# Layer 0's out projection by column halves with kept weights, its LayerNorms on VectorE alone, and normalised rows in the residual's tiles

## The chip, the cores and the metric

The kernel runs on one core of a Trainium2 chip. Its engines work side by side and meet through semaphores: TensorE (PE) multiplies, with a queue of its own for weight loads (PEld); VectorE (DVE), ScalarE (ACT) and GpSimd (POOL) do elementwise work; SyncE (SP) issues most of the DMAs. Each engine takes its instructions strictly in the order in which they were written for it. The metric is the device time of one execution in microseconds (us), as a median of runs.

## The reference

Two layers of a diffusion backbone on 256 context tokens and 256 latent tokens of width 1024. What matters here is layer 0 from its output projection on; both streams pass through the same weights, with modulation rows of their own:

```
y     = mixed @ w_out                                   # 1024 x 1024
x_mid = LN(alpha * x + ada2 * y) * ln1_g + ln1_b
h2    = LN(x_mid) * (1 + ada4) + ada3                   # "modulate"
f     = (silu(h2 @ wg) * (h2 @ wu)) @ wd                # 1024 -> 2816 -> 1024
x     = LN(alpha * x_mid + ada5 * f) * ln2_g + ln2_b
h     = LN(x) * (1 + ada1) + ada0                       # layer 1 begins, then h @ w_in
```

Everything is float32. LN is a LayerNorm without gain and bias.

## The kernel before, in words

The 512 tokens are four tiles of 128 rows: tiles 0 and 1 are the context (stream s=0), tiles 2 and 3 the latent tokens (s=1). A row tile is two SBUF tiles of 128x512. A float32 product is made of three matmuls (`mm3`, L223 to L225): high by high, high by low, low by high part. `load_w` brings a block of a weight, here 512 rows by 256 columns (512 KB), with a DMA on SP's queue; ACT then makes the high part (L216, tile "hi") and DVE the low part (L217, tile "lo"). The weights stand in rings of tiles: raw 5, hi 3, lo 3, and in the phase "ff" 3, 1 and 1 more, so that four pairs of hi and lo exist there. A split has to wait until TensorE has read the pair that it overwrites.

A row-major product (`tok_group`) fills one PSUM bank "PM" for two token tiles and a group g of 256 output columns; there are four such groups and three PM banks. Its evacuation is `add_residual`: DVE multiplies the bank with the gate row (L1040), POOL adds the residual (L1041), DVE takes the LayerNorm statistics (L1042). `post_ln` then closes the statistics (the power -1/2 is POOL's, L231, "rs") and applies LN, gain and bias: the first 512 columns on DVE in two instructions (L1054, L1055), the last 512 on ACT (L1050) and POOL (L1051, L1052). With quick=True, which `out_last` uses in layer 1, add and both halves are DVE's.

`modulate` is next. `normalise` takes statistics again (L247) and makes the normalised row, half on ACT (L361), half on DVE (L362), into tiles of tag "B". TensorE transposes it in eight column blocks (L374, PSUM tiles "PX", three of them). Each block is scaled and shifted into a tile of the ring "sg" (ACT L382 and DVE L380 in turn), and split into high part (ACT L383) and low part (DVE L384); both go into tiles "H", which the next matmuls read.

The first place is L1690 to L1693: stream by stream, `out_proj` runs groups g=0 to 3 over two tiles (so w_out is read twice), then post LN and modulate. The second is the end of `ffn` (L1151 to L1161): for each stream the last 10 of 22 blocks of the down projection, again in four groups, into new tiles "xn" of tag "in", then post LN and modulate for layer 1, whose projection by w_in follows.

The ring "sg" has four tiles. A tile of a ring is handed out in the order in which the program asks for it; who asks waits until the last reader of the tile's former content is done. Within such bounds a scheduler writes each engine's order when the kernel is built; at run time nothing is reordered.

Of the kernel before, what the change touches and what calls it, by code (L numbers as in the profile page):

```python
# [10 lines left out]
F32 = mybir.dt.float32  # L11
# [85 lines left out]
def hybrid_backbone(ctx: ExitStack, tc: tile.TileContext, A, out, dbg=None, stop=None):  # L97
# [28 lines left out]
    def tt(tag, dt=F32, n=512):  # L126
        t = S["main"].tile([128, 512], dt, name=tag, tag=tag, bufs=TAGS[tag])
        return t if n == 512 else t[:, :n]

    def ht(dt=F32R):  # L130
        return hpool.tile([128, 512], dt, name="H")
# [101 lines left out]
    def ln_open(k):  # L233
        return cc(24, "bst", bufs=4).rearrange("p (a b) -> p a b", b=6)[:, :k]
# [15 lines left out]
    def load_row(src, tag):  # L250
        r = []
        for i in range(2):
            t = tt(tag)
            nc.gpsimd.dma_start(t, bcast_rows(src[512 * i:512 * i + 512], 512))
            r.append(t)
        return r
# [99 lines left out]
    def normalise(x):  # L356
        mu, rs = ln_stats(x)
        nb = cc(1, "nb", bufs=4)
        nc.vector.scalar_tensor_tensor(nb, mu, -1.0, rs, op0=OP.mult, op1=OP.mult)
        z = [tt("B") for _ in range(2)]  # L360
        nc.scalar.activation(z[0], x[0], AF.Identity, scale=rs, bias=nb)  # L361
        nc.vector.tensor_scalar(z[1], x[1], mu, rs, op0=OP.subtract, op1=OP.mult)  # L362
        return z
# [72 lines left out]
    def tok_group(src, c0, act, evac, tiles, n=256, kk=8):  # L436

        h, lo = act
        tiles = list(tiles)
        banks = [pmt() for _ in range(0, len(tiles), 2)]  # L440
        ps = {t: banks[i // 2][:, 256 * (i % 2):256 * (i % 2) + n] for i, t in enumerate(tiles)}
        for k0 in range(0, kk, 4):
            kc = min(4, kk - k0)
            w = load_w(src, 128 * k0, kc, c0, n)
            for i, t in enumerate(tiles):
                for k in range(kc):
                    sl = slice(128 * t, 128 * t + 128)

                    mm3(ps[t], (h[k0 + k][:, sl], lo[k0 + k][:, sl]), (w[0][:, k, :], w[1][:, k, :]),
                        k0 + k == 0 and i % 2 == 0, k0 + k == kk - 1, skip_group_check=True)  # L450
        for t in tiles:
            evac(t, ps[t])
# [583 lines left out]

    def add_residual(z, g, p, r, ax, st, quick=False):
        c = slice(256 * (g % 2), 256 * (g % 2) + 256)
        zc = z[g // 2][:, c]
        nc.vector.tensor_tensor(zc, p, r[g // 2][:, c], op=OP.mult)  # L1040
        (nc.vector if quick else nc.gpsimd).tensor_tensor(zc, zc, ax[g // 2][:, c], op=OP.add)  # L1041
        nc.vector.bn_stats(st[:, g, :], zc)  # L1042

    def post_ln(z, st, rows, quick=False):
# [12 lines left out]
    def times_alpha(x):  # L1057
        for i in range(2):
            nc.scalar.activation(x[i], x[i], AF.Copy, scale=ALPHA)
        return x  # L1060

    def out_proj(l, m, ax, s, rows):
        tiles = (2 * s, 2 * s + 1)
        zs = {t: [tt("in") if l == 0 else ht(F32) for _ in range(2)] for t in tiles}
        st = {t: ln_open(4) for t in tiles}
        r = load_row(S["adarows"][0, l, 1 - s, :], "C")
        for g in range(4):
            tok_group(A["w_out"][l], 256 * g, m, lambda t, p: add_residual(zs[t], g, p, r, ax[t], st[t]), tiles)
        for t in tiles:
            post_ln(zs[t], st[t], rows)  # L1070
        return zs

    def out_last(m, ax, rows, after):
# [22 lines left out]
    def ffn(act, xm, fill, plan, after):  # L1096

        wg, wu, wd = A["ffd_wg"][0], A["ffd_wu"][0], A["ffd_wd"][0]
        zs = {}
        hid = {}  # L1100

        def up(fp, sl):
            sgs = [None, None]

            def ev_g(i, p):
                s = sg()
                sgs[i] = s
                nc.scalar.activation(s[:, sl], p[:, sl], AF.Silu)  # L1108

            def ev_u(i, p):  # L1110
                s = sgs[i]
                nc.vector.tensor_tensor(s[:, sl], s[:, sl], p[:, sl], op=OP.mult)
                if fp + i not in hid:
                    hid[fp + i] = (tt("B", F32R), tt("C", F32R))
                hi, lo = hid[fp + i]
                nc.scalar.activation(hi[:, sl], s[:, sl], AF.Copy)
                nc.vector.tensor_tensor(lo[:, sl], s[:, sl], hi[:, sl], op=OP.subtract)
            col_pair(wg, 128 * fp, act, ev_g, sl)
            col_pair(wu, 128 * fp, act, ev_u, sl)

        def take(at):
            for _ in range(plan.count(chr(65 + at))):
                fill.pop(0)()
        for half, (f0, f1) in enumerate(((0, 12), (12, 22))):
            for fp in range(f0, f1, 2):
                if fp == 0:
                    for sl in (slice(0, 256), slice(256, 512)):
                        for f in (0, 2):
                            up(f, sl)
                elif fp > 2:  # L1130
                    up(fp, slice(0, 512))
                if fp == 4:
                    for t in range(4):
                        times_alpha(xm[t])
                take(fp // 2)
            n = f1 - f0
            hh = ([hid[f][0] for f in range(f0, f1)], [hid[f][1] for f in range(f0, f1)])
            if half == 0:
                rows = {j: load_row(S["adarows"][1, 0, j, :], "in") for j in range(2)}
                for t in range(4):  # L1140
                    zs[t] = xm[t]
                for g in range(4):
                    def ev(t, p):
                        c = slice(256 * (g % 2), 256 * (g % 2) + 256)
                        k = sg()[:, :256]
                        nc.vector.tensor_tensor(k, p, rows[0 if t >= 2 else 1][g // 2][:, c], op=OP.mult)
                        nc.gpsimd.tensor_tensor(zs[t][g // 2][:, c], zs[t][g // 2][:, c], k, op=OP.add)
                    tok_group(wd[128 * f0:128 * f1], 256 * g, hh, ev, range(4), kk=n)
                    take(11 + g)
        ln2 = load_row(A["ln2_g"][0], "B"), load_row(A["ln2_b"][0], "B")  # L1150
        for s in range(2):  # L1151
            tiles = (2 * s, 2 * s + 1)
            st = {t: ln_open(4) for t in tiles}
            xn = {t: [tt("in") for _ in range(2)] for t in tiles}
            for g in range(4):
                tok_group(wd[128 * f0:128 * f1], 256 * g, hh,
                          lambda t, p: add_residual(xn[t], g, p, rows[1 - s], zs[t], st[t]), tiles, kk=n)
                take(15 + 4 * s + g)
            for t in tiles:
                post_ln(xn[t], st[t], ln2)  # L1160
            after(s, xn)  # L1161

# [487 lines left out]
    def load_x(t, q):  # L1652
        src = A["ctx"][0, 128 * t:128 * t + 128, :] if t < 2 else A["x"][0, 128 * (t - 2):128 * (t - 2) + 128, :]
        x = [tt("in") for _ in range(2)]
        for i in range(2):
            q.dma_start(x[i], src[:, 512 * i:512 * i + 512])
        return x

    xsave = dram.tile([2, 128, D], F32, name="xsave")
    with phase("main") as S["main"]:  # L1660
# [24 lines left out]
        with phase("ff") as ff, deeper(ff, 3, 1, 1):  # L1685
            ff.tile([128, 16], F32, name="shift")
            act = new_act()
            rows = load_row(A["ln1_g"][0], "B"), load_row(A["ln1_b"][0], "B")
            xm = {}
            for s in range(2):  # L1690
                ax = {t: times_alpha(load_x(t, nc.gpsimd)) for t in (2 * s, 2 * s + 1)}
                xm.update(out_proj(0, m, ax, s, rows))
                modulate(0, xm, 3, s, act)  # L1693
            for t in range(4):
                for i in range(2):
                    dump("xmid0", xm[t][i], lambda o: o[128 * t:128 * t + 128, 512 * i:512 * i + 512])
            if stop == "mid":
                return
            act2 = []

            def after(s, x):
                if not act2:
                    act2.extend(new_act())
                for t in x:
                    for i in range(2):
                        dump("x0", x[t][i], lambda o: o[128 * t:128 * t + 128, 512 * i:512 * i + 512])
                        if t >= 2:
                            nc.gpsimd.dma_start(xsave[t - 2, :, 512 * i:512 * i + 512], x[t][i])
                modulate(1, x, 0, s, act2)
            ffn(act, xm, fill, "CDFGHIJKLMNOPR", after)  # L1710
# [54 lines left out]
```

## Time and profile before

| | |
|---|---|
| median of 3 runs | 1908.01 us (1906.63 to 1915.2) |
| profiled execution, its own time | 1905.72 us |
| its span | 1903.9 us, mean TensorE clock 0.964 |
| TensorE busy | 1777.5 us, 93% of the span |
| VectorE busy | 1249.4 us, 66% |
| ScalarE busy | 835.0 us, 44% |
| GpSimd busy | 515.6 us, 27% |
| DMA | 337.89 MB, 177 GB/s in the mean |

TensorE is busy nearly everywhere, so what counts is where it is not, and what it waits for there. A share of busy time over the whole span says nothing on the two places of the change; windows and timelines of those places do. A row of a timeline has start, length, engine, line, operation, output and inputs and, in brackets, how long the engine stood idle before it and what released it. The granted clock is the share of full speed (1.00 is 2.4 GHz, 0.50 is 1.2 GHz).

### The profile page before, as it was taken

What the parts mean: (1) busy time and instruction counts of PE and PEld (TensorE: products, weight loads), DVE (VectorE), ACT (ScalarE), POOL (GpSimd) and SP (SyncE); (2) the same over time, 40 slices, a digit from 0 to 9 for tenths busy, and PEclk for the clock granted to TensorE, in tenths of its full rate; (3) what the DMA queues carried; (4) which work ended last, traced back from release to release, by engine and by line L of the source; (5) the groups of instructions that cost most, each with busy time, mean ns of one, the idle gap of its engine ahead of it and who ended that gap; (6) DMA issues with size and microseconds to landing.
All of it is one profiled execution on the core that took longest, in us unless ns stands there. A gap on an engine that the chain in (4) does not pass through costs nothing. (4 is left out here: it accounts for less than half of the span.)

```text
span 1903.9 us, 29201 instructions
## 1 busy us (share of the span) xinstructions
PE 1777.5 (93%) x10822; PEld 1411.8 (74%) x10822; DVE 1249.4 (66%) x2029; ACT 835.0 (44%) x1430; POOL 515.6 (27%) x532
## 2 busy tenths in 40 slices
PE   6899989999999979999999989989989899999994
PEld 3777977788777968799788978878978475664731
DVE  5777767765555876757767965676867475655722
ACT  3454554434443463221233454564644374544620
POOL 2353536652202720112102730046504000001001
PEclk8998989999999979999999989999999899999997
DMA  8424321123213736545666543323528699779994
GB/s 303 138 90 144 110 89 56 46 66 118 84 54 105 228 99 189 183 149 175 228 211 202 165 139 100 112 89 106 165 70 297 210 371 343 275 273 383 377 376 179
DMA packets 243934, 337.89 MB, mean 177 GB/s; under 512 B 16008, under 2 KB 158864, under 8 KB 243784
## 3 DMA queue, kind: packets, MB, share of 16 engines
q1 hardware_dynamic: 235896, 318.86, 50.5%
q0 software_dynamic: 6128, 13.99, 2.4%
q10 hardware_dynamic: 1760, 3.09, 0.5%
q8 instruction: 87, 1.43, 0.3%
q14 instruction: 63, 0.52, 0.1%
HBM read 333.77 MB, written 2.12 MB: 176 GB/s over the span
## 5 line engine op out<-in xcount | busy, mean ns | idle before, releaser
L217 DVE TENSOR_TENSOR lo<-raw,hi 128x1024 fp32r<-128x1024 f32 (+1 forms) x370 | 456.0, 1239 | 161.8 <-ACT hi L216 159.9
L216 ACT ACTIVATE hi<-raw 128x1024 fp32r<-128x1024 f32 (+1 forms) x370 | 368.3, 1003 | 433.9 <-PE PM L225 170.2
L223 PE MATMUL PM<-H,hi 128*128 128x512 f32 (+1 forms) x1104 | 388.0, 354 | 7.5 <-ACT sg L1108 2.9
L224 PE MATMUL PM<-H,hi 128*128 128x512 f32 (+1 forms) x1104 | 386.7, 351 | 1.2 <-DVE H L384 1.1
L225 PE MATMUL PM<-H,lo 128*128 128x512 f32 (+1 forms) x1104 | 384.9, 351 | 0.0
L223 PEld LDWEIGHTS PM<-H,hi 128*128 128x128 f32 x1104 | 211.3, 192 | 44.3 <-issue 4.4
L224 PEld LDWEIGHTS PM<-H,hi 128*128 128x128 f32 x1104 | 211.5, 192 | 32.2 <-issue 2.0
L225 PEld LDWEIGHTS PM<-H,lo 128*128 128x128 f32 x1104 | 210.5, 191 | 31.8 <-issue 2.7
L332 DVE SCALAR_TENSOR_TENSOR ad<-raw,silu,ad 128x512 f32<-128x512 f32 x208 | 177.9, 875 | 35.9 <-issue 15.1
L223 PE MATMUL PM<-hi,H 128*128 128x256 f32 x432 | 127.2, 295 | 4.1 <-ACT in L529 4.1
L224 PE MATMUL PM<-lo,H 128*128 128x256 f32 x432 | 126.7, 293 | 1.9 <-DVE lo L217 1.9
L225 PE MATMUL PM<-hi,H 128*128 128x256 f32 x432 | 126.1, 292 | 0.0
L1024 POOL TENSOR_TENSOR B<-B,sg 128x512 f32<-128x512 f32 (+1 forms) x48 | 62.7, 1318 | 216.4 <-DVE sg L1023 199.6
L1521 POOL TENSOR_TENSOR yl<-sg,yh 128x512 fp32r<-128x512 f32 x17 | 24.6, 1448 | 349.9 <-ACT yh L1520 330.8
L809 POOL TENSOR_TENSOR C<-C,in 128x512 f32<-128x512 f32 (+1 forms) x64 | 82.7, 1317 | 74.8 <-ACT C L808 48.8
L1396 PE MATMUL PM<-raw,xs 128*64 128x512 f32 (+3 forms) x448 | 99.9, 565 | 0.0
L223 PE MATMUL PM<-hi,B 128*128 128x256 f32 x352 | 98.6, 280 | 0.0
L225 PE MATMUL PM<-hi,C 128*128 128x256 f32 x352 | 98.1, 279 | 0.0
L224 PE MATMUL PM<-lo,B 128*128 128x256 f32 x352 | 98.0, 278 | 0.0
L223 PEld LDWEIGHTS PM<-hi,H 128*128 128x128 f32 x432 | 86.3, 200 | 5.7 <-ACT in L529 4.3
L224 PEld LDWEIGHTS PM<-lo,H 128*128 128x128 f32 x432 | 86.4, 200 | 4.1 <-DVE lo L217 2.2
L225 PEld LDWEIGHTS PM<-hi,H 128*128 128x128 f32 x432 | 86.4, 200 | 0.8 <-issue 0.8
(444 smaller groups left out, 3561.8 us busy)
## 6 DMA issues: line engine op xcount, KB each, us to landing
raw<-in_w_ada_dram SPq DMA_DIRECT2D x80, 512.0 KB, 4.3
raw<-in_moe_wd_dram SPq DMA_DIRECT2D x80, 512.0 KB, 7.0
raw<-in_w_gate_dram SPq DMA_DIRECT2D x64, 512.0 KB, 3.6
raw<-in_moe_wg_dram SPq DMA_DIRECT2D x60, 512.0 KB, 8.2
raw<-in_moe_wu_dram SPq DMA_DIRECT2D x60, 512.0 KB, 9.9
raw<-in_w_in_dram SPq DMA_DIRECT2D x54, 512.0 KB, 3.7
raw<-in_ffd_wd_dram SPq DMA_DIRECT2D x28, 512.0 KB, 3.5
raw<-in_ffd_wg_dram SPq DMA_DIRECT2D x26, 512.0 KB, 3.8
```

What stands on the lines that cost most here:

```text
L216: nc.scalar.activation(h[:, :m], raw[:, :m], AF.Copy)
L217: (nc.vector if ahead else nc.gpsimd).tensor_tensor(l[:, :m], raw[:, :m], h[:, :m], op=OP.subtract)
L223: nc.tensor.matmul(o, ah, bh, start=start, stop=False, **kw)
L224: nc.tensor.matmul(o, ah, bl, start=False, stop=False, **kw)
L225: nc.tensor.matmul(o, al, bh, start=False, stop=stop, **kw)
L332: nc.vector.scalar_tensor_tensor(acc[j], part, sc, acc[j], op0=OP.mult, op1=OP.add)
L809: nc.gpsimd.tensor_tensor(E[:, xt], E[:, xt], X[:, xt], op=OP.mult)
L1024: nc.gpsimd.tensor_tensor(mixed[c][:, xt], mixed[c][:, xt], s[:, xt], op=OP.add)
L1396: nc.tensor.matmul(po[g, :w.shape[-1]], x[:, c, :], w, start=(c < k), stop=(c + k >= kk), tile_position=(0, g.start))
L1521: nc.gpsimd.tensor_tensor(yl, y, yh, op=OP.subtract)
```

## The change

1. `normalise` writes its rows into tiles of tag "in" instead of "B".
2. Layer 0's `out_proj` takes columns 0 to 511 (g=0, 1) for all four token tiles, with one load of the weights. It then loads the four weight blocks of columns 512 to 1023 and keeps them split, and runs g=2, 3 for s=0, then for s=1. There are 8 loads of w_out instead of 16.
3. In `out_proj` the adds of g=2, 3 and the whole post LN are DVE's (quick), and modulate of a stream follows its post LN through `after`. The x and ctx rows of all four tiles are loaded and scaled ahead of it.
4. At the end of `ffn` the tiles "xn" are gone: the sum is made in place in zs, and the product before it goes into a tile of the ring "sg". The add of g=3 and the whole post LN are DVE's.

```diff
@@ -357,7 +357,7 @@
         mu, rs = ln_stats(x)
         nb = cc(1, "nb", bufs=4)
         nc.vector.scalar_tensor_tensor(nb, mu, -1.0, rs, op0=OP.mult, op1=OP.mult)
-        z = [tt("B") for _ in range(2)]
+        z = [tt("in") for _ in range(2)]
         nc.scalar.activation(z[0], x[0], AF.Identity, scale=rs, bias=nb)
         nc.vector.tensor_scalar(z[1], x[1], mu, rs, op0=OP.subtract, op1=OP.mult)
         return z
@@ -1036,9 +1036,11 @@
 
     def add_residual(z, g, p, r, ax, st, quick=False):
         c = slice(256 * (g % 2), 256 * (g % 2) + 256)
-        zc = z[g // 2][:, c]
-        nc.vector.tensor_tensor(zc, p, r[g // 2][:, c], op=OP.mult)
-        (nc.vector if quick else nc.gpsimd).tensor_tensor(zc, zc, ax[g // 2][:, c], op=OP.add)
+        zc, k = z[g // 2][:, c], z[g // 2][:, c]
+        if z is ax:
+            k = sg()[:, :256]
+        nc.vector.tensor_tensor(k, p, r[g // 2][:, c], op=OP.mult)
+        (nc.vector if quick else nc.gpsimd).tensor_tensor(zc, k, ax[g // 2][:, c], op=OP.add)
         nc.vector.bn_stats(st[:, g, :], zc)
 
     def post_ln(z, st, rows, quick=False):
@@ -1059,15 +1061,32 @@
             nc.scalar.activation(x[i], x[i], AF.Copy, scale=ALPHA)
         return x
 
-    def out_proj(l, m, ax, s, rows):
-        tiles = (2 * s, 2 * s + 1)
-        zs = {t: [tt("in") if l == 0 else ht(F32) for _ in range(2)] for t in tiles}
-        st = {t: ln_open(4) for t in tiles}
-        r = load_row(S["adarows"][0, l, 1 - s, :], "C")
-        for g in range(4):
-            tok_group(A["w_out"][l], 256 * g, m, lambda t, p: add_residual(zs[t], g, p, r, ax[t], st[t]), tiles)
-        for t in tiles:
-            post_ln(zs[t], st[t], rows)
+    def out_proj(m, ax, rows, after):
+
+
+        w_out = A["w_out"][0]
+        zs = {t: [tt("in") for _ in range(2)] for t in range(4)}
+        st = {t: ln_open(4) for t in range(4)}
+        r = [load_row(S["adarows"][0, 0, 1 - s, :], "C") for s in range(2)]
+        for g in range(2):
+            tok_group(w_out, 256 * g, m, lambda t, p: add_residual(zs[t], g, p, r[t // 2], ax[t], st[t]), range(4))
+        w = {(g, k0): load_w(w_out, 128 * k0, 4, 256 * g, 256) for g in (2, 3) for k0 in (0, 4)}
+        for s in range(2):
+            tiles = (2 * s, 2 * s + 1)
+            for g in (2, 3):
+                ps = pmt()
+                for i, t in enumerate(tiles):
+                    o = ps[:, 256 * i:256 * i + 256]
+                    for k in range(8):
+                        wh, wl = w[g, k & 4][:2]
+                        sl = slice(128 * t, 128 * t + 128)
+                        mm3(o, (m[0][k][:, sl], m[1][k][:, sl]), (wh[:, k & 3, :], wl[:, k & 3, :]),
+                            k == 0 and i == 0, k == 7, skip_group_check=True)
+                for i, t in enumerate(tiles):
+                    add_residual(zs[t], g, ps[:, 256 * i:256 * i + 256], r[s], ax[t], st[t], quick=True)
+            for t in tiles:
+                post_ln(zs[t], st[t], rows, quick=True)
+            after(s, zs)
         return zs
 
     def out_last(m, ax, rows, after):
@@ -1151,14 +1170,13 @@
         for s in range(2):
             tiles = (2 * s, 2 * s + 1)
             st = {t: ln_open(4) for t in tiles}
-            xn = {t: [tt("in") for _ in range(2)] for t in tiles}
             for g in range(4):
                 tok_group(wd[128 * f0:128 * f1], 256 * g, hh,
-                          lambda t, p: add_residual(xn[t], g, p, rows[1 - s], zs[t], st[t]), tiles, kk=n)
+                          lambda t, p: add_residual(zs[t], g, p, rows[1 - s], zs[t], st[t], quick=g == 3), tiles, kk=n)
                 take(15 + 4 * s + g)
             for t in tiles:
-                post_ln(xn[t], st[t], ln2)
-            after(s, xn)
+                post_ln(zs[t], st[t], ln2, quick=True)
+            after(s, {t: zs[t] for t in tiles})
 
 
 
@@ -1686,11 +1704,8 @@
             ff.tile([128, 16], F32, name="shift")
             act = new_act()
             rows = load_row(A["ln1_g"][0], "B"), load_row(A["ln1_b"][0], "B")
-            xm = {}
-            for s in range(2):
-                ax = {t: times_alpha(load_x(t, nc.gpsimd)) for t in (2 * s, 2 * s + 1)}
-                xm.update(out_proj(0, m, ax, s, rows))
-                modulate(0, xm, 3, s, act)
+            xm = out_proj(m, {t: times_alpha(load_x(t, nc.gpsimd)) for t in range(4)}, rows,
+                          lambda s, zs: modulate(0, zs, 3, s, act))
             for t in range(4):
                 for i in range(2):
                     dump("xmid0", xm[t][i], lambda o: o[128 * t:128 * t + 128, 512 * i:512 * i + 512])
```

Two places of DVE's order and one of TensorE's show what moves. In what follows PM is a PSUM bank of a product, PX one of transposes, "in" a row tile.

The first is DVE in the out projection, after the normalised rows of s=0 (L362). Before:

```order
L362 TENSOR_SCALAR B_5768<-in_5453,mv_5759,rs_5761 128x512
L362 TENSOR_SCALAR B_5783<-in_5455,mv_5774,rs_5776 128x512
L217 TENSOR_TENSOR lo_6345<-raw_6342,hi_6344 128x1024
L1042 BN_STATS bst_5858<-in_5855 128x6
L1042 BN_STATS bst_5859<-in_5857 128x6
L380 TENSOR_SCALAR sg_5796<-PX_5793,adac0_119 128x256
L238 BN_AGGR mv_6132<-bst_5858 128x2
L238 BN_AGGR mv_6145<-bst_5859 128x2
```

After, where the g=2 and g=3 banks of s=1 are PM_5968 and PM_6023:

```order
L362 TENSOR_SCALAR in_5894<-in_5465,mv_5885,rs_5887 128x512
L359 SCALAR_TENSOR_TENSOR nb_5906<-mv_5900,rs_5902 128x1
L362 TENSOR_SCALAR in_5909<-in_5467,mv_5900,rs_5902 128x512
L1042 TENSOR_TENSOR in_5469<-PM_5968,C_5482 128x256
L1042 TENSOR_TENSOR in_5471<-PM_5968,C_5482 128x256
L1042 TENSOR_TENSOR in_5469<-PM_6023,C_5482 128x256
L1042 TENSOR_TENSOR in_5471<-PM_6023,C_5482 128x256
L1043 TENSOR_TENSOR in_5469<-in_5469,in_5453 128x256
L1043 TENSOR_TENSOR in_5471<-in_5471,in_5459 128x256
L1043 TENSOR_TENSOR in_5469<-in_5469,in_5453 128x256
L1043 TENSOR_TENSOR in_5471<-in_5471,in_5459 128x256
L380 TENSOR_SCALAR sg_5922<-PX_5919,adac0_119 128x256
```

Four multiplications and four adds of s=1 now stand between s=0's rows and the first of its blocks (L380); before it were a split and two statistics.

The second is DVE at the end of `ffn`. Before, PM_9834 and PM_9919 are the banks g=2 and g=3 of s=1, evacuated ahead of s=0's modulate (L380) or between its blocks:

```order
L359 SCALAR_TENSOR_TENSOR nb_9596<-mv_9590,rs_9592 128x1
L1040 TENSOR_TENSOR in_9661<-PM_9834,in_7464 128x256
L1040 TENSOR_TENSOR in_9663<-PM_9834,in_7464 128x256
L217 TENSOR_TENSOR lo_10155<-raw_10152,hi_10154 128x1024
L1042 BN_STATS bst_9658<-in_9661 128x6
L362 TENSOR_SCALAR B_9584<-in_9141,mv_9575,rs_9577 128x512
L1042 BN_STATS bst_9659<-in_9663 128x6
L362 TENSOR_SCALAR B_9599<-in_9143,mv_9590,rs_9592 128x512
L380 TENSOR_SCALAR sg_9612<-PX_9609,adac1_120 128x256
L1040 TENSOR_TENSOR in_9661<-PM_9919,in_7464 128x256
L1040 TENSOR_TENSOR in_9663<-PM_9919,in_7464 128x256
```

After, PM_9598, PM_9685 and PM_9772 are the banks g=0, 1, 2 of s=1, and L1042 is the multiplication:

```order
L384 TENSOR_TENSOR H_9506<-sg_9571,H_9498 128x256
L384 TENSOR_TENSOR H_9507<-sg_9578,H_9499 128x256
L1042 TENSOR_TENSOR sg_9677<-PM_9598,in_7402 128x256
L384 TENSOR_TENSOR H_9508<-sg_9585,H_9500 128x256
L1042 TENSOR_TENSOR sg_9681<-PM_9598,in_7402 128x256
L384 TENSOR_TENSOR H_9509<-sg_9592,H_9501 128x256
L1042 TENSOR_TENSOR sg_9764<-PM_9685,in_7402 128x256
L1044 BN_STATS bst_9596<-in_5468 128x6
L1042 TENSOR_TENSOR sg_9768<-PM_9685,in_7402 128x256
```

The multiplications of s=1's first three groups have moved behind all but the last blocks of s=0's modulate, since their products take tiles of the ring "sg" after it.

TensorE at that place. Before, the transposes (L374) stand in four lots among the last matmuls of s=1's g=3 (PM<-hi,C) and the first of w_in (PM<-H,hi); here the third and the fourth:

```order
L225 MATMUL PM<-hi,C 128x256
L374 MATMUL PX<-cst,B 128x128 x6
L223 MATMUL PM<-H,hi 128x256 x2
L223 MATMUL PM<-hi,H 128x256
L374 MATMUL PX<-cst,B 128x128 x2
L224 MATMUL PM<-H,hi 128x256
```

After, all sixteen stand in one piece ahead of s=1's g=3:

```order
L224 MATMUL PM<-lo,B 128x256
L225 MATMUL PM<-hi,C 128x256
L374 MATMUL PX<-cst,in 128x128 x16
L223 MATMUL PM<-hi,B 128x256
L224 MATMUL PM<-lo,B 128x256
```

What follows L374 is now the group g=3 itself, in a bank that g=0 held before, and no matmul of w_in stands between the transposes.

## Rows read from the trace of the kernel before

**Rows 1.** The page, busy time of each engine

```profile
PE 1777.5 (93%) x10822; PEld 1411.8 (74%) x10822; DVE 1249.4 (66%) x2029; ACT 835.0 (44%) x1430; POOL 515.6 (27%) x532
```

**Rows 2.** Windows: start:end, length, busy us of PE, PEld, DVE, ACT, POOL, clock, DMA

```profile
645.00:665.00 20.00, 20.00 (x172) 20.00 (x171) 19.11 (x38) 8.85 (x9) 15.18 (x13) 1.00 0.56 167
...
670.00:675.00 5.00, 2.68 (x11) 2.18 (x11) 5.00 (x14) 3.64 (x8) 1.71 (x2) 0.50 0.44 134
...
695.00:700.00 5.00, 2.96 (x14) 2.96 (x15) 1.94 (x6) 2.85 (x6) 0.00 (x0) 0.50 0.01 2
```

**Rows 3.** Timeline of PE, out projection to the first up matmuls

```profile
619.95 0.28 PE L223 MATMUL PM<-hi,C 128*128 128x256 f32 x1
...
665.06 0.28 PE L225 MATMUL PM<-hi,B 128*128 128x256 f32 x1
668.08 1.61 PE L374 MATMUL PX<-cst,B 128*128 128x128 f32 x6 [2.75 <-ACT B L361]
...
697.04 0.58 PE L223 MATMUL PM<-H,hi 128*128 128x256 f32 x1 [2.87 <-ACT sg L1108]
```

**Rows 4.** Timeline of DVE, same stretch

```profile
667.55 0.16 DVE L359 SCALAR_TENSOR_TENSOR nb<-mv,rs 128x1 f32<-128x1 f32 x1 [0.37 <-POOL rs L231]
...
669.93 1.21 DVE L217 TENSOR_TENSOR lo<-raw,hi 128x1024 fp32r<-128x1024 f32 x1
...
671.73 0.52 DVE L380 TENSOR_SCALAR sg<-PX,adac 128x256 f32<-128x256 f32 x1
...
672.52 0.74 DVE L1054 SCALAR_TENSOR_TENSOR in<-in,mv,B 128x512 f32<-128x512 f32 x1
...
678.97 3.29 DVE L384 TENSOR_TENSOR H<-sg,H 128x256 fp32r<-128x256 f32 x3
...
694.67 1.42 DVE L384 TENSOR_TENSOR H<-sg,H 128x256 fp32r<-128x256 f32 x4
```

**Rows 5.** Timeline of ACT, same stretch

```profile
667.22 1.52 ACT L361 ACTIVATE B<-in,nb,rs 128x512 f32<-128x512 f32 x2 [0.79 <-DVE nb L359]
...
688.19 1.14 ACT L1059 ACTIVATE in<-in 128x512 f32<-128x512 f32 x2
689.24 1.04 ACT L216 ACTIVATE hi<-raw 128x1024 fp32r<-128x1024 f32 x1
690.18 1.00 ACT L382 ACTIVATE sg<-PX,adac 128x256 f32<-128x256 f32 x2
```

**Rows 6.** Windows at the end of the feed-forward, columns as in Rows 2

```profile
1102.00:1108.00 6.00, 0.47 (x5) 0.26 (x3) 5.39 (x12) 1.30 (x3) 4.41 (x7) 0.76 0.72 206
1108.00:1112.00 4.00, 3.77 (x17) 3.17 (x18) 2.22 (x7) 3.43 (x8) 0.46 (x1) 0.51 0.63 224
```

**Rows 7.** Timeline of DVE, end of the feed-forward

```profile
1053.62 0.76 DVE L1040 TENSOR_TENSOR in<-PM,in 128x256 f32<-128x256 f32 x2
...
1100.20 4.51 DVE L217 TENSOR_TENSOR lo<-raw,hi 128x1024 fp32r<-128x1024 f32 x2
1104.64 1.27 DVE L247 BATCH_NORM_STATS2 bst<-in 128x6 f32<-128x512 f32 x2
...
1106.88 0.16 DVE L359 SCALAR_TENSOR_TENSOR nb<-mv,rs 128x1 f32<-128x1 f32 x1 [0.54 <-POOL rs L231]
...
1115.04 0.43 DVE L384 TENSOR_TENSOR H<-sg,H 128x256 fp32r<-128x256 f32 x1 [0.48 <-ACT H L383]
```

**Rows 8.** Timeline of PE, end of the feed-forward

```profile
1107.95 1.61 PE L374 MATMUL PX<-cst,B 128*128 128x128 f32 x6 [5.54 <-ACT B L361]
...
1111.83 0.40 PE L224 MATMUL PM<-H,hi 128*128 128x256 f32 x1
```

**Rows 9.** Timeline of POOL, end of the feed-forward

```profile
1086.47 2.56 POOL L1041 TENSOR_TENSOR in<-in 128x256 f32<-128x256 f32 x2
...
1096.57 3.60 POOL L1051 TENSOR_TENSOR in<-in,B 128x512 f32<-128x512 f32 x2
1100.13 3.50 POOL L1052 TENSOR_TENSOR in<-in,B 128x512 f32<-128x512 f32 x2
```

## The prediction

> **What bounds the kernel now.** I read the page first: TensorE is busy 93% of the span, no other engine over 66% [rows 1]. So only stretches in which TensorE stands still, or runs slowly, can give time or take it. The windows show two at the places of the change.
>
> Stage 1 is the end of the out projection. Its 384 matmuls run from 619.95 to 665.06 without a gap, 0.1178 us apart [rows 3], and need 45.2 us. Then TensorE waits 2.75 us for the first normalised rows (ACT L361) and is busy 2.68 us of 5 at a clock of 0.50 [rows 2, 3], fed in pieces by the modulate of s=0, then of s=1. The up matmuls after s=1's modulate begin at 697.04 [rows 3]. That instant, 77.1 us after 619.95, is my mark for stage 1. The bound is DVE: 19.11 us busy of 20 before 665, all 5 of 5 behind it [rows 2].
>
> Stage 2 is the end of the feed-forward. I count from the evacuation of s=0's last group at 1053.62 [rows 7]. TensorE works through s=1's down projection and s=0's part of w_in, then waits 5.54 us for s=1's rows (ACT L361) and runs the start of the next stretch at 0.51 [rows 6, 8]. It is back in w_in at 1111.83 [rows 8], 58.2 us after 1053.62: the mark for stage 2. The order of DVE and POOL decides here; the statistics of s=1's last columns wait for POOL's L1051 and L1052 [rows 7, 9].
>
> **The change, part by part.** The eight w_out loads that go, with 4 MB, are worth 0: TensorE waits for no weight between 619.95 and 665.06 [rows 3]. The eight splits that go with them free DVE and ACT only inside that stretch. Loading and scaling all x and ctx rows early puts four scalings of 0.57 us (two take 1.14 [rows 5]) ahead of other work of ACT; I take 0, at most 1 us if a load is late. POOL's sixteen gain and bias instructions and ACT's L1050 go. DVE gains two instructions of 0.66 us (0.74 long [rows 4], 0.08 overlapped) for each of eight half rows, 10.6 us, and 12 adds at 0.34 (four instructions on 256 columns last 1.42 [rows 4]), 4.1 us: 8.0 us in stage 1, which has eight of the adds, and 6.7 in stage 2.
>
> Stage 1. The four kept weight blocks take all four pairs of hi and lo. They are last read at 36.7, 39.6, 42.4 and 45.2 us, since s=1's two groups are the last four steps of 24 matmuls, 2.83 us each. So the next four splits, of the up weights, can't run sooner, and DVE's order has them inside s=0's post LN and statistics; the last begins after ACT's high part (1.04 [rows 5]) at 46.2 and takes 1.14 (1.21 long [rows 4]). With aggregation, power on POOL and two small instructions, 1.1 us, the factors nb stand at 48.5; before they stood at 667.55, 47.6 [rows 4]. So 0.9 us is lost, and the long LN on DVE is covered by the wait for those slots.
>
> From there DVE's order up to the nb of s=1 holds 2 L362 and 4 L380 at 0.46 (L380 is 0.52 long [rows 4]), 24 on 256 columns at 0.34 (8 multiplications and adds, 4 statistics, 8 L384, and 4 aggregations taken at half of it, 7.5 together), 8 instructions of post LN at 0.66 (5.3), 2 splits (2.3), 4 statistics on 512 columns at 0.61 (two last 1.27 [rows 7]; 2.4) and 1.2 for small ones with the power: 21.5 us, so nb is there at 70.0. ACT then makes two L361 (1.52) and four scalings (2.28) before its first L382, 73.8. In the trace the mark follows the first L382 (690.18) by 6.86 us [rows 3, 5]; so it comes at 80.7, against 77.1: **+3.6 us**. Bounds: if DVE's splits wait for TensorE and POOL's remaining adds slow it, +5.5; if DVE runs ahead into the waits of the modulate, and the scalings hide, -2.
>
> Stage 2. s=1's products now use the ring sg, whose four tiles are taken after s=0's modulate. So the evacuations of its g=0 to 2 stand behind that modulate on DVE. There are three PM banks: g=3 of s=1 can't begin before the first of them is empty, and behind it in TensorE's queue stands all of w_in. From 1053.62 TensorE has 180 matmuls, 21.2 us. DVE has, up to nb of s=0, four multiplications and adds (1.4), two statistics (0.7), 8 post LN instructions (5.3), 4 statistics on 512 (2.4), six splits at 1.14 and two of half the width (8.0), and aggregations and two powers (1.7): nb at about 19.5, 1.1 us before the second tile's. From nb to the last block of a modulate the trace has 8.6 us (1106.88 to 1115.47 [rows 7]), in part at half clock; with a split that now stands between the two tiles' factors, 9.0. So the bank is free at about 28.5. TensorE, done at 21.2 except for transposes, **waits some 6 to 7 us that are new**; before, the transposes stood between matmuls of g=3 and w_in. g=3 needs 60 matmuls, 7.1 us: 35.6.
>
> DVE's chain for s=1 from there: multiplications, adds, statistics 2.0, first four post LN instructions 2.6, five splits 5.7 of which one stands behind the copies (L532), and those wait for 96 matmuls of w_in, 11.3 us. So the copies end at 12.4, and 4 post LN instructions (2.6), a split (1.1), 4 statistics (2.4), aggregation and power (1.2) follow: nb at 19.7. TensorE's 120 matmuls of w_in end at 14.1, so it waits again. The mark followed nb (1106.88) by 4.95 us [rows 7, 8]: 35.6 + 19.7 + 4.95 = 60.3, against 58.2: +2.1. After a wait of 5.54 us the clock was 0.51 for 4 us [rows 6, 8], which would add 2 to g=3; I take half: **+3.1 us**. Bounds: -6, if the evacuations hide, as in the faster rival; +8, if g=3 runs wholly at half clock.
>
> Sum: 1905.7 + 3.6 + 3.1 = 1912.4 against the profiled execution; the median lies 2.3 above that execution, which gives 1914.7, so **1915 us**. What cannot be told from no change is 0.5%, 9.5 us: 1898.5 to 1917.5.
>
> Contention, weighed: three L384 beside POOL's L1051 and L1052 took 3.29 us, four alone 1.42 [rows 4]; two splits beside L1052 took 4.51 instead of 2.4 [rows 7]. The Trainium skill, "Trainium Architecture — The Big Picture", section "What this means for kernel authors", says that VectorE and GpSimd share a port pair with an exclusive lock. The trace agrees in these two places. That rule speaks for the change and is the first rival below.
>
> **Rivals.** Faster: without POOL's long instructions the DVE chains are shorter than before, not longer. For it: 2.2 us of excess in stage 1 and 2.1 in stage 2 by those rows; in stage 2 POOL's last add for s=1 came only at 1086.47, behind other work (its row has no idle time before it), and L1051 and L1052 held the last statistics until 1104.64 [rows 7, 9]. If the new wait at g=3 were hidden too, the 5.54 us go [rows 8], and stage 1 gains 4.3 (the excess of 2.2 and as much of half clock): 1908.0 - 9.9 = 1898. Against it: the change puts 14.7 us on DVE where 4.3 of excess go, and the evacuations behind the modulate are not a matter of speed.
>
> Slower: the clock. Place: g=3 of s=1 after the new wait, and the up matmuls after stage 1. Price: 60 matmuls wholly at half clock take 7.1 us more, of which my sum has 1, thus +6; it decides if the wait is over the 5.54 us after which 0.51 was granted [rows 6, 8], and mine is 6 or more. The up matmuls behind stage 1 would add about 2, as 4 us at half clock do: 1915 + 6 + 2 = 1923. For it: 0.50 after each wait of stage 1 [rows 2]; against it: the sixteen transposes keep TensorE partly at work during the wait. The Trainium skill, "TensorE: Matmul & The Clock Gate", section "What's actually happening", says that the throttled clock is the default and activity releases it; the trace agrees with both levels, 0.50 and 1.00.
>
> No effect at all: the slots, not DVE, set stage 1 both ways, and stage 2's wait is only moved from s=1's rows to g=3: 1908.
>
> **Chances.** Forecast and no effect together are the case within 0.5%: 0.42 (0.30 and 0.12). Slower, 0.36, is the clock rival and the upper part of my bounds; a sum along one chain leaves out the waits that it does not see. Faster, 0.22. The likeliest one's own range is 1909 to 1919; for 8 in 10 I go from 1897, the faster rival, to 1926, past the slower one.
>
> **What would show it.** Right: a wait of TensorE of 5 to 8 us before a down matmul L223, released by DVE's L1042, some 21 us after s=0's last group; the first L361 of s=0 in stage 1 a microsecond later than 2.0 us after the out projection's end; L382 of s=1 about 74 us after the projection's start; another wait of 5 us or so for L361 in w_in. Wrong: no such wait at g=3, or DVE idle before s=0's nb in stage 1; then the faster rival holds. If a clock of 0.5 stands over all of g=3, the slower one does.

## The result, and the profile after

The changed kernel takes 1923.12 us (median of 6 runs, 1922.58 to 1924.36); the kernel before took 1909.98 us over the 6 runs beside it. The ratio is 1.0067, with a 95% interval of 1.0055 to 1.0078: slower by 0.7%. The forecast was 1915 us, within 1897 to 1926; the time is that which the slower rival gave, 1923. The profiled execution took 1924.36 us, 18.6 more than that of before. Single executions scatter by some us, and the executions profiled lay low for before and high for after, so the two traces show 5.5 us more than the medians do (18.6 against 13.1).

Where the time goes can be read by following the same TensorE instruction through both traces. Up to the out projection it starts 1.9 us later after the change; both traces part near 158 us, where nothing was changed. Behind stage 1 it is 5.2 late, at the feed-forward's end 6.3, behind stage 2 14.3, and at the end 18.9. So stage 1 costs 3.3 us, stage 2 about 8, and some 4 come later, in layer 1; about 1 lies between the two stages.

**Stage 1.** The timeline of PE after the change, as in [rows 3]:

```profile
621.84 0.28 PE L223 MATMUL PM<-hi,C 128*128 128x256 f32 x1
...
666.95 0.28 PE L225 MATMUL PM<-hi,B 128*128 128x256 f32 x1
672.61 0.69 PE L374 MATMUL PX<-cst,in 128*128 128x128 f32 x2 [5.39 <-ACT in L361]
...
702.13 0.58 PE L223 MATMUL PM<-H,hi 128*128 128x256 f32 x1 [2.78 <-ACT sg L1127]
```

The projection still runs without a gap, 621.84 to 666.95, and the mark, 702.13, lies 80.3 us after its first matmul, against 77.1. The wait for s=0's rows has grown from 2.75 to 5.39 us. DVE, as in [rows 4, 5]: the evacuation of s=0's last bank, the last of the four splits for which the kept blocks hold the slots, the first factors of s=0 and of s=1. Below it ACT: the high part for that split, and its first scalings of s=1's blocks:

```profile
655.96 0.76 DVE L1042 TENSOR_TENSOR in<-PM,C 128x256 f32<-128x256 f32 x2 [3.56 <-PE PM L225]
...
669.57 1.17 DVE L217 TENSOR_TENSOR lo<-raw,hi 128x1024 fp32r<-128x1024 f32 x1
...
671.55 0.16 DVE L359 SCALAR_TENSOR_TENSOR nb<-mv,rs 128x1 f32<-128x1 f32 x1 [0.50 <-POOL rs L231]
...
692.24 0.15 DVE L359 SCALAR_TENSOR_TENSOR nb<-mv,rs 128x1 f32<-128x1 f32 x1
```

```profile
667.26 1.06 ACT L216 ACTIVATE hi<-raw 128x1024 fp32r<-128x1024 f32 x1 [0.35 <-DVE bst L247]
...
695.93 1.00 ACT L382 ACTIVATE sg<-PX,adac 128x256 f32<-128x256 f32 x2
```

Counted from the first matmul, s=0's two factors stand at 49.7 and 50.4 (before at 47.1 and 47.6; I had 48.5, set against the second), the first of s=1 at 70.4 (I had 70.0), and L382 at 74.1 (73.8). The windows show how DVE's load has moved: the first 34.1 us, up to s=0's last bank, and from there to the first factor of s=1; columns as in [rows 2]. After the change, then before it, split at the same 34.1 us:

```profile
621.84:655.94 34.10, 34.10 (x291) 34.10 (x290) 17.18 (x30) 6.01 (x7) 13.52 (x17) 1.00 0.45 140
655.94:692.24 36.30, 25.18 (x184) 23.69 (x183) 35.52 (x81) 14.76 (x24) 6.40 (x8) 0.84 0.25 73
```

```profile
619.95:654.05 34.10, 34.10 (x291) 34.10 (x290) 28.06 (x45) 16.83 (x20) 23.10 (x26) 1.00 0.75 249
654.05:684.59 30.54, 23.72 (x158) 21.98 (x157) 29.31 (x60) 15.11 (x25) 21.91 (x19) 0.78 0.41 119
```

Up to s=1's factors DVE has less work than before, 52.7 us against 57.4. But of the first 34.1 us it stands idle 16.9, before 6.0: it waits for TensorE's banks and for ACT's high parts. From s=0's last bank on it is full, 35.5 of 36.3 us, and TensorE waits for it.

**Stage 2.** DVE, as in [rows 7]: the last group of s=0, the two evacuations of the first bank of s=1, which stand among s=0's last blocks, and the first factors of s=1:

```profile
1059.88 0.76 DVE L1042 TENSOR_TENSOR sg<-PM,in 128x256 f32<-128x256 f32 x2
...
1087.43 0.42 DVE L1042 TENSOR_TENSOR sg<-PM,in 128x256 f32<-128x256 f32 x1
...
1088.09 0.42 DVE L1042 TENSOR_TENSOR sg<-PM,in 128x256 f32<-128x256 f32 x1
...
1116.90 0.16 DVE L359 SCALAR_TENSOR_TENSOR nb<-mv,rs 128x1 f32<-128x1 f32 x1 [0.61 <-POOL rs L231]
```

TensorE in the same stretch, as in [rows 8]; the rows from 1080.31 on are the transposes of s=0, 1088.57 is the first matmul of s=1's g=3:

```profile
1080.31 0.55 PE L374 MATMUL PX<-cst,in 128*128 128x128 f32 x3
1082.14 0.55 PE L374 MATMUL PX<-cst,in 128*128 128x128 f32 x3 [1.28 <-ACT in L361]
1083.13 2.02 PE L374 MATMUL PX<-cst,in 128*128 128x128 f32 x8 [0.44 <-ACT sg L382]
1085.44 0.69 PE L374 MATMUL PX<-cst,in 128*128 128x128 f32 x2 [0.30 <-ACT sg L382]
1088.57 0.58 PE L223 MATMUL PM<-hi,B 128*128 128x256 f32 x1 [2.44 <-DVE sg L1042]
...
1117.96 1.61 PE L374 MATMUL PX<-cst,in 128*128 128x128 f32 x6 [5.13 <-ACT in L361]
...
1132.87 0.50 PE L223 MATMUL PM<-H,hi 128*128 128x512 f32 x1 [1.46 <-ACT hi L216]
```

The last row has its counterpart in the kernel before:

```profile
1119.59 0.50 PE L223 MATMUL PM<-H,hi 128*128 128x512 f32 x1 [1.46 <-ACT hi L216]
```

TensorE ended s=1's g=2 at about 1080 and began g=3 at 1088.57, 28.7 us after s=0's last group; I had put that at 28.5. In the 8.6 us between it does 16 transposes and waits 4.5 us, 2.44 of them for L1042. The windows give the clock; columns as before:

```profile
1086.00:1091.00 5.00, 2.56 (x12) 2.44 (x12) 4.89 (x15) 1.37 (x5) 3.08 (x5) 0.50 0.00 0
...
1118.00:1124.00 6.00, 6.00 (x28) 5.80 (x29) 2.81 (x6) 4.30 (x10) 0.00 (x0) 0.50 0.01 2
```

g=3 begins at 0.50 and is done at 1097.85, 9.3 us instead of 7.1; and the second wait, for s=1's rows, is still there, followed by 0.50 for 6 us. The first matmul of w_in on 512 columns, which has the same work ahead of it in both kernels, starts 73.0 us after s=0's last group (1132.87), before 66.0 (1119.59): 7.0 us.

### The profile page after: what moved, and what is told of

The parts are those of the page before. It is cut to its first block, busy times and chain, and to the rows that moved or that the text cites. A ratio compares the mean times of both kernels' runs of the same rounds, so it can differ in the third digit from the quotient of the medians.

```text
span 1922.6 us, 29159 instructions
## 1 busy us (share of the span) xinstructions
PE 1786.9 (93%) x10822; PEld 1419.8 (74%) x10822; DVE 1240.7 (65%) x2041; ACT 819.0 (43%) x1414; POOL 469.6 (24%) x504
## 5 line engine op out<-in xcount | busy, mean ns | idle before, releaser
L216 ACT ACTIVATE hi<-raw 128x1024 fp32r<-128x1024 f32 (+1 forms) x362 | 360.1, 1002 | 474.8 <-PE PM L225 187.8
L217 DVE TENSOR_TENSOR lo<-raw,hi 128x1024 fp32r<-128x1024 f32 (+1 forms) x362 | 438.9, 1219 | 178.2 <-ACT hi L216 171.3
L225 PE MATMUL PM<-H,lo 128*128 128x512 f32 (+1 forms) x1104 | 387.1, 353 | 0.0
L223 PEld LDWEIGHTS PM<-H,hi 128*128 128x128 f32 x1104 | 212.8, 194 | 45.1 <-issue 6.1
L225 PEld LDWEIGHTS PM<-H,lo 128*128 128x128 f32 x1104 | 212.2, 193 | 31.6 <-issue 2.7
L225 PE MATMUL PM<-hi,H 128*128 128x256 f32 x432 | 125.6, 291 | 0.0
L225 PE MATMUL PM<-hi,C 128*128 128x256 f32 x352 | 98.9, 281 | 0.0
L225 PEld LDWEIGHTS PM<-hi,H 128*128 128x128 f32 x432 | 86.1, 199 | 0.8 <-issue 0.8
```

Source lines behind the costliest of these rows:

```text
L216: nc.scalar.activation(h[:, :m], raw[:, :m], AF.Copy)
L217: (nc.vector if ahead else nc.gpsimd).tensor_tensor(l[:, :m], raw[:, :m], h[:, :m], op=OP.subtract)
L223: nc.tensor.matmul(o, ah, bh, start=start, stop=False, **kw)
L225: nc.tensor.matmul(o, al, bh, start=False, stop=stop, **kw)
```

## The experiments

Each version ran beside the kernel before, whose median lay between 1909.5 and 1910.6 us there. A diff shows the lines that carry an edit, not all of it. Beside the ratio I give two differences for each run: how much later than in the trace of before the same TensorE instruction starts, over stage 1 (615 to 712 us) and over stage 2 (1040 to 1150 us). For the changed kernel they are +3.3 and +8.1. A single trace scatters by about 2 us in stage 2, as the first run shows.

**1. Only the out projection changed.** The feed-forward's end is that of before, with its rows in tiles of tag "B".

```diff
-            post_ln(zs[t], st[t], ln2, quick=True)
+            post_ln(xn[t], st[t], ln2)
```

> Only layer 0's out projection by halves with its LayerNorms on DVE; the end of the feed-forward as before. Theory (the ring of product tiles costs most, in the feed-forward's end; the out projection costs 3 to 4 us): 1914 us, the up matmuls behind s=1's modulate 80 us after the projection's first matmul, no wait of TensorE for L1042 later. Rival (the out projection's order causes the whole loss): 1922 us.

1916.81 us, ratio 1.0037 (1.0022 to 1.0053); stage 1 +2.8, stage 2 +2.3. So the out projection costs about half of the whole, and stage 1 repeats. In stage 2 TensorE's order is that of before, and so is its wait, 5.5 us; yet it loses 2.3 us. The clock tells why. This run, then the kernel before, whose clock of 0.51 from 1108 to 1112 us stands in [rows 6]:

```profile
1110.00:1112.00 2.00, 1.77 (x8) 1.17 (x9) 0.65 (x2) 1.43 (x4) 0.37 (x1) 0.50 0.97 333
1112.00:1114.00 2.00, 2.00 (x11) 2.00 (x10) 1.57 (x5) 1.97 (x7) 0.00 (x0) 0.50 0.26 101
1114.00:1116.00 2.00, 2.00 (x11) 2.00 (x11) 1.85 (x5) 1.52 (x4) 0.61 (x1) 0.50 0.04 8
...
1124.00:1126.00 2.00, 2.00 (x8) 1.71 (x7) 2.00 (x2) 0.37 (x1) 0.00 (x0) 0.50 0.04 4
```

```profile
1112.00:1114.00 2.00, 2.00 (x19) 2.00 (x19) 1.85 (x6) 1.58 (x5) 0.52 (x1) 1.00 0.03 8
...
1120.00:1122.00 2.00, 1.79 (x10) 1.34 (x9) 2.00 (x3) 1.43 (x2) 0.00 (x0) 1.00 0.00 0
```

Behind the wait half clock lasts 6 us here and 4 in the trace of before, with the same work; that is 1.0 us of the loss. After the next wait, 1.46 us for a split in both, the clock falls to 0.50 again here and stays at 1.00 there: another 1.2. So the trace of before is some 2 us short in this place, against this one, and part of the 8.1 of the changed kernel is of this kind (its clock is 0.57 from 1134 to 1138 us).

**2. Only the feed-forward's end changed.**

```diff
+            k = sg()[:, :256]
-                post_ln(xn[t], st[t], ln2)
+                post_ln(zs[t], st[t], ln2, quick=True)
```

The diff is against the kernel before.

> Only the end of the feed-forward is changed (sum in place, product in the ring sg, LayerNorm on DVE); the out projection as before. Theory (ring): 1918 to 1921 us, with the wait for L1042 ahead of s=1's g=3 and half clock behind it. Rival (the two parts cost only together, or the loss lies in the out projection): 1911 us.

1915.43 us, ratio 1.0026 (1.0014 to 1.0038); stage 1 -0.2, stage 2 +8.6. Less than the theory's 1918, though the stage repeats to half a us; the view of waits is that of the changed kernel:

```profile
PE PX L374 <- ACT in L361: 6.3, 2, 5.1
PE PM L223 <- DVE sg L1042: 2.4, 1, 2.4
```

(In such a row stand total, number and longest of the waits.) The two parts add up within their intervals: 0.37 and 0.26 against 0.67%.

**3. The changed kernel with a ring of its own for the products.**

```diff
-            k = sg()[:, :256]
+            k = S["kp"].tile([128, 256], F32, name="kp", tag="kp", bufs=4)
```

> The whole change, but the products of the in-place sum take four tiles of 128x256 of their own instead of tiles of sg. Theory (ring): no wait for L1042 ahead of g=3, clock 1.00 there, 6 to 9 us less than the changed kernel: 1914 to 1917 us. Rival (the LayerNorm on DVE alone makes s=1's chain late): 1921 us or more.

1917.43 us, ratio 1.0041 (1.0026 to 1.0056); stage 1 +3.2, stage 2 +2.9. DVE's order takes s=1's first banks ahead of s=0's modulate again, and the wait for L1042 is gone:

```profile
PE PM L223 <- DVE v L532: 3.4, 1, 3.4
PE PM L223 <- ACT hi L216: 2.2, 2, 2.0
PE PX L374 <- ACT sg L382: 1.8, 1, 1.8
PE PX L374 <- ACT in L361: 1.4, 4, 0.7
```

The long wait for L361 has gone with it. In its place stands a new one, for the copies L532 out of the banks of w_in. g=3 runs at a clock of 1.00 (up to 1088 us), as expected. The median falls by 5.7 us (5.0 by the two ratios), a little short of the 6 to 9 expected.

**4. The changed kernel with the old LayerNorm at the feed-forward's end.**

```diff
-                post_ln(zs[t], st[t], ln2, quick=True)
+                post_ln(zs[t], st[t], ln2)
```

The add of g=3 goes back to POOL too.

> The whole change, but at the feed-forward's end the add of g=3 and the second half of the post LN go back to POOL and ACT; the products stay in sg. Theory (ring): the wait for L1042 stays, 1921 to 1926 us. Rival (LayerNorm on DVE): 1915 us or less.

1925.92 us, ratio 1.0089 (1.0071 to 1.0107); stage 2 +11.5. The rival is dead: without DVE's LayerNorm the stage is worse, with one wait for L361 of 9.7 us. So the LayerNorm on DVE gains some 3 us in stage 2 of these traces, and the sum in place, through the ring, loses more (5.2 by run 3).

**5. w_out loaded again for each stream.**

```diff
-        w = {(g, k0): load_w(w_out, 128 * k0, 4, 256 * g, 256) for g in (2, 3) for k0 in (0, 4)}
+                tok_group(w_out, 256 * g, m, lambda t, p: add_residual(zs[t], g, p, r[s], ax[t], st[t], quick=True), tiles)
```

> The whole change, but the weight blocks of columns 512 to 1023 are not kept: each stream loads them again (12 loads of w_out instead of 8). Theory that the kept blocks hold the slots of the next splits and so make s=0's rows late: the first rows of s=0 come 4 to 4.5 us after the projection's end instead of 5.4, stage 1 costs 1 to 2 us instead of 3, 1921 us. Rival, that s=1's multiplications and adds and the long LayerNorm on DVE cost it: stage 1 as in the changed kernel, 3 us, 1923 us.

1918.25 us, ratio 1.0048 (1.0029 to 1.0067); stage 1 +5.3, stage 2 +5.5. Stage 1 is worse, not better: s=0's rows come later still (a wait of 6.6 us), so my expectation falls, and the rival's with it. But loading again also brings DVE four more splits, and one of them (1.1 us) stands between s=0's last bank and its factors, which come at 50.9 instead of 49.7. So the run does not settle what the held slots cost. The median is lower than the changed kernel's all the same, by what the trace gives back between the stages, in stage 2 and in layer 1.

**6. POOL's LayerNorm in the out projection.**

```diff
-                post_ln(zs[t], st[t], rows, quick=True)
+                post_ln(zs[t], st[t], rows)
```

The adds of g=2 and 3 go back to POOL too.

> The whole change, but in the out projection adds of g=2, 3 and the second half of the post LN are POOL's and ACT's again. Theory (kept blocks' slots): stage 1 still 3 us or more late, 1923 to 1926 us. Rival (LayerNorm on DVE costs stage 1): stage 1 no later than in the kernel before, 1919 us.

1921.59 us, ratio 1.0055 (1.0035 to 1.0076); stage 1 +3.4, stage 2 +8.7. Nothing moves in stage 1: s=0's factors come at 49.6 and 51.9. Taking the LayerNorm back from DVE gains nothing there.

**7. The kernel before with DVE's LayerNorm at the feed-forward's end.**

```diff
-                post_ln(xn[t], st[t], ln2)
+                post_ln(xn[t], st[t], ln2, quick=True)
```

The add of g=3 is DVE's as well.

> The kernel before, with nothing changed but that at the feed-forward's end the add of g=3 and the whole post LN are DVE's; the sum stays in tiles of its own (xn), so no product takes a tile of sg. Theory (the ring costs, the LayerNorm on DVE gains): no wait for L1042, s=1's rows 2 to 5 us earlier, 1905 to 1908 us. Rival (LayerNorm on DVE costs): 1912 us or more.

1905.73 us, ratio 0.9988 (0.9976 to 1.0000); stage 1 -0.6, stage 2 -1.2. The wait of 5.5 us for s=1's rows has become

```profile
PE PX L374 <- ACT B L361: 1.8, 2, 1.6
```

This is what the change's idea is worth without the sum in place: about 0.1%, with an interval that ends at no change.

**8. The kernel before with DVE's LayerNorm in the out projection.**

```diff
-            post_ln(zs[t], st[t], rows)
+            post_ln(zs[t], st[t], rows, quick=True)
```

The adds of g=2 and 3 are DVE's as well.

> The kernel before, with nothing changed but that in the out projection the adds of g=2, 3 and the whole post LN are DVE's; the streams still follow one another and w_out is loaded for each. Theory (kept blocks and order by halves cost stage 1): 1907 to 1911 us, the up matmuls no later than before. Rival (LayerNorm on DVE costs it): 1914 us.

1907.63 us, ratio 0.9994 (0.9977 to 1.0012); stage 1 -0.2, stage 2 +2.0 (half clock for nearly 6 us and once more after the next wait, as in run 1). DVE's LayerNorm alone is free there: s=0's rows come after a wait of 4.75 us instead of 2.75, without harm.

**9. The second run with the ring of the third.** Only the feed-forward's end is changed, with tiles of their own for the products.

```diff
-            k = sg()[:, :256]
+            k = S["kp"].tile([128, 256], F32, name="kp", tag="kp", bufs=4)
```

> The out projection as before; the end of the feed-forward as changed (sum in place, LayerNorm on DVE), but with four tiles of 128x256 of their own for the products. It differs from the run e2_ffn_alone by that ring alone. Theory (ring): no wait for L1042, the stretch from 1040 to 1150 us costs 0 to 1 us instead of 8.6, 1906 to 1910 us. Rival (the sum in place costs by itself): 1914 us.

1915.06 us, ratio 1.0037 (1.0022 to 1.0052); stage 2 +4.8. Against run 2 the stage gives back 3.8 us, and its waits are

```profile
PE PM L223 <- DVE v L532: 4.1, 1, 4.1
PE PM L223 <- ACT hi L216: 2.1, 2, 1.9
```

The time is no better than run 2's: in this trace another 4.1 us come between 1300 and 1370 us, outside both stages, and were not followed. So the theory holds for the wait but not for the sum: with the ring aside, the sum in place still costs 4.8 us in the stage against a gain of 1.2 in run 7. In DVE's timeline splits that wait for ACT (0.91 and 1.27 us, at 1096.65 and 1099.48) stand inside s=1's LayerNorm, and the copies L532 behind it (1105.61). Why the order comes out so with the sum in place was not separated further.

**10. Both LayerNorms on DVE, nothing else** (runs 7 and 8 together; the diff is theirs).

> The kernel before with the LayerNorms of layer 0 and the late adds on DVE at both places, no halves, no sum in place. Theory: the gains of the two single runs add up, -0.1 to -0.3%, 1903 to 1908 us. Rival (the two single differences were noise, or DVE is too full): 1910 us or more.

1907.04 us, ratio 0.9991 (0.9977 to 1.0005); stage 1 -0.3, stage 2 -1.2. The gains do not add up to more than run 7's; this version beats the changed kernel by 0.8%, the kernel before by nothing that can be told.

**11. Three column groups for all tiles, one by stream.**

```diff
-        for g in range(2):
+        for g in range(3):
```

and (3,) for (2, 3) in the kept part. The adds of g=2 go back to POOL with it.

> The whole change, but columns 0 to 767 are done for all four tiles first, and only the last 256 columns by stream with kept weights (two blocks). s=0's rows come later than in the changed kernel, and only one group of s=1 is left for DVE behind the projection's end. Theory (the work of s=1 that DVE has left behind the projection's end sets the up matmuls): stage 1 costs 1 to 2.5 us, 1922 us. Rival (the lateness of s=0's rows sets them): stage 1 costs 5 us or more, 1925 us.

1920.58 us, ratio 1.0060 (1.0042 to 1.0079); stage 1 +3.3, stage 2 +8.2. Between the two expectations. s=1's factors stand 66.8 us after the projection's first matmul, 3.6 earlier than in the changed kernel, but s=0's rows are so late that TensorE waits 13.1 us for them, and the mark stands at 79.6, against 80.3. So earlier factors of s=1 alone do not bring the mark back to 77.1.

**12. The changed kernel stream by stream.**

```diff
-        for g in range(2):
-            tok_group(w_out, 256 * g, m, lambda t, p: add_residual(zs[t], g, p, r[t // 2], ax[t], st[t]), range(4))
+            for g in range(4):
+                tok_group(w_out, 256 * g, m, lambda t, p: add_residual(zs[t], g, p, r[s], ax[t], st[t], quick=g >= 2), tiles)
```

> The whole change, but the out projection goes stream by stream, all four groups of s=0 and then of s=1, with w_out loaded for each; adds of g=2, 3 and LayerNorm stay on DVE, the early x loads stay. Theory (the order by halves costs stage 1): stage 1 within 0.7 us of the kernel before, the feed-forward's end as in the changed kernel, 1918 to 1920 us. Rival (the early loads and scalings, or DVE's LayerNorm, cost it): stage 1 still 3 us late, 1923 us.

1919.92 us, ratio 1.0055 (1.0036 to 1.0074); stage 1 +3.5, stage 2 +8.2. Stage 1 stays 3.5 us late without the halves, as the rival said, but by another way than it gave. s=0's rows are early now, and the scheduler has put the first of its transposes ahead of the last 48 matmuls of s=1's g=3:

```profile
666.09 0.55 PE L374 MATMUL PX<-cst,in 128*128 128x128 f32 x3 [3.38 <-ACT in L361]
667.42 0.38 PE L223 MATMUL PM<-hi,C 128*128 128x256 f32 x1 [0.79 <-DVE in L1042]
```

TensorE waits inside the projection and runs some 3.5 us of it at half clock; its last matmul starts at 52.6 us instead of 45.1, DVE evacuates s=1's last bank at 53.5 (run 8: 47.2), and s=1's factors stand at 70.2, as in the changed kernel, after a wait of TensorE of 9.7 us. So the run does not clear the order by halves: it has a loss of its own.

## Why the prediction was right, and where it was off

**Direction and range** were right, the size was not: the sum added 6.7 us to the time before, and 13.1 were measured.

**Stage 1** (+3.6 forecast, +3.3 measured, 2.8 to 3.5 in the six other runs with the new out projection or its early loads, run 5 apart). The chain along DVE came out within half a us at s=1's factors, at L382 and at the mark. That it fits so well is partly luck: s=0's first factors came 1.2 us later than I had them, the stretch from there to s=1's took 20.7 us instead of 21.5, and the one from L382 to the mark 6.2 instead of 6.9. The first step was wrong in its reason. I had DVE wait for the slots of the kept weights, with the long LayerNorm hidden in that wait. The slots do hold ACT back (before the first of the four high parts it waits 14.5 us, until a matmul of L225), but DVE never waits for them: ACT's last high part is done at 46.5, and DVE, busy without a gap since s=0's last bank, comes to its split only at 47.7, which is the 1.2 us. (The first L361 comes 4.7 us after the projection's end, where I had announced 3.) What the trace shows in place of the wait is the idle time ahead of that bank: the order by halves leaves DVE idle for 16.9 us there instead of 6.0, and puts the rest of its work behind. No run isolates this. DVE's LayerNorm alone is not the cost (run 8), and run 12, meant to take the halves out, lost as much because TensorE's order changed with it; which of its differences from run 8 (tiles of the rows, early loads and scalings, place of modulate) brought that order stays open.

**Stage 2** (+3.1 forecast, +7.0 measured up to the first matmul on 512 columns). The step that I built on is right and shown: s=1's products wait for the ring sg, g=3 starts at 28.7 instead of 28.5, and with a ring of their own the wait goes (runs 3 and 9). That ring is worth 5.0 us in the whole change (run 3, by the ratios); where only the feed-forward's end is changed the stage gains 3.8 and the time nothing (runs 2 and 9). The wait is shorter than "6 to 7 us": 4.5 in four pieces, of which 2.44 are the wait for L1042 that I had announced at 5 to 8. Two terms were mis-sized. The first is the mark itself: I had TensorE back in w_in 4.95 us after the factors, as before, but in the changed order 24 matmuls of s=0's w_in, which before ran ahead of the wait, stand behind it, among the transposes and at half clock. By my mark, the return to w_in, stage 2 costs only 1.5 us (1119.58 is 59.7 us after s=0's last group, before 58.2). From the factors to the first matmul on 512 columns it takes 16.0 us (1116.90 to 1132.87) instead of 12.7 (1106.88 to 1119.59): 3.3 us that I did not count. The second is the factors: 57.0 us after s=0's last group against 55.3, with 1.0 allowed for the clock; g=3 took 9.3 instead of 7.1.

**Layer 1** was left at nothing. In the traces about 4 us more come there (2.8 up to 1300 us, 1.4 from 1370 to 1435). The first appears in the changed kernel's trace alone, so it is scatter as far as these runs tell. The second, 1.4 to 2.5 us, stands in all six traces that have kept weight blocks, and not in the seven others, which are 0.4 to 1.7 us early there against before. In the six with kept blocks TensorE's order differs at that place: two matmuls of the attention scores (L948) wait 4.2 to 5.2 us for ACT (L952), and the transposes behind them up to 2.5 for DVE; before, these two stand ahead of a wait of 4.0 for DVE (L1180), and the transposes wait 1.9. Why kept blocks bring this order was not looked for.

**The rivals.** The faster one is refuted as a whole and right in part: DVE's LayerNorm does shorten s=1's chain, and without the sum in place the 5.5 us wait shrinks to 1.6 (run 7), but the gain is 1.2 us of the 5.5 it promised, and nothing in stage 1. The slower one gave the right time by luck, with the wrong place: half clock cost 2.2 us at g=3, not 7.1, and its condition, a wait over 5.54 us, was not met when the clock fell there. Of the rest, 24 matmuls more stand behind the second wait, which that rival did not name, in 6 us of half clock instead of 4.

**Contention.** The excess in [rows 4] and [rows 7], some 2 us in each place, was not won back in full in either: with POOL's long instructions gone and nothing else changed, the feed-forward's end gained 1.2 us (run 7) and the out projection 0.2 (run 8).

## What to carry to other kernels

A temporary taken from a ring orders its user behind all who took from the ring before: ask which engine's queue then holds the evacuation that a PSUM bank waits for. When a wait is removed by putting work on one engine, sum that engine's queue up to the instruction that TensorE waits for, not its share of the span, and ask when each piece of that work becomes ready: idle time ahead of it counts like work. When two orders are compared at a mark, count the work that each has done by then.

## What the runs showed of the hardware that was not expected

After the same wait of 5.5 us the same stretch of w_in ran at 0.50 for 4 us in one execution and for 6 in another, and after the same wait of 1.46 us the next ran at 1.00 in the one and at 0.50 in the other: 2.3 us between executions of the same order (run 1). Executions of the kernel before ran from 1901.8 to 1916.5 us among 23 side by side, so that differences under 0.2% need the interval, not two traces. Ahead of s=1's g=3 the clock fell from 1.00 to 0.50 at about 1083 us, after TensorE had done six transposes in 3 us with waits of 1.28 and 0.44 us; the longer wait of 2.44 us came behind the fall.
